# Hybrid streaming-encoder layer on one core: the convolution branch's two transpositions through DRAM with one contiguous store and four loads of 2 KB pieces each

## The chip, the core and the metric

The kernel runs on one core of a Trainium2 chip. TensorE (PE) multiplies matrices and transposes into PSUM, VectorE (DVE), ScalarE (ACT) and GpSimd (POOL) do the elementwise work, and SyncE (SP) issues most of the DMAs. Each engine carries out its own instructions in the order in which they were built; semaphores make one engine wait for another or for a DMA. The metric is the time in microseconds (us) of one execution of the program on the device; the median of several runs is compared. A profiled execution has its own time and a span, which is the stretch from the first to the last instruction that the trace shows.

## What is computed

One layer of a streaming encoder with 512 tokens and 1024 channels, in float32. Four token mixers (differential attention A, forgetting attention F, a convolution branch C, a short gated convolution D) share one input projection, are gated, summed and projected; cross-attention and a gated MLP follow. The change is in branch C:

```python
c_a, c_g = jnp.split(c_u + b_glu[l], 2, axis=-1)
yc = _dwconv_causal(c_a * jax.nn.sigmoid(c_g), conv_dw[l]) + conv_dw_b[l]   # 31 taps, 512 channels
yc = jax.nn.silu(_layer_norm(yc, conv_ln_g[l], conv_ln_b[l]))               # mean and variance over channels
...
br = jnp.stack([ya, yf, yc, ys], axis=2)
proj = jnp.einsum('bsnc,ncd->bsnd', br, w_branch[l])
```

The convolution runs along tokens, so channels lie on partitions; the layer norm needs sums over channels, so there tokens lie on partitions. The branch is turned twice: channels to tokens before the norm and back after it.

## The kernel before

Every matrix product is made of three float32r products (high part by high part, high by low, low by high), so each weight block is loaded by SP into one of two `wr` buffers (`load_raw`, L176), rounded to its high part `wh` by ACT (L190), and its low part `wl` is made by DVE (L191). `run_blocks` walks through a list of such blocks and keeps three of them ahead. A block is 24 products of 128x512 on PE. There are four `wh` and four `wl` buffers, so the cast of a block waits until PE has finished the block four places ahead of it.

Work that is not a weight block is written as generators (`bg.add`), which are advanced between blocks, up to two at a time; each yields a cost and a waiting time. `conv_norm_task` is one of them. The final order of the instructions on every engine is made when the kernel is built, by a scheduler that simulates the engines; on the chip that order is fixed.

Around the change the blocks on PE are, in this order: the last block of branch D's output (`y8b`), four blocks of the values of attention A (`v_jobs`: products into four PSUM banks, two tagged `av` and two tagged `mm`), then the query and key projections of the first head (`qk_jobs`, L772 to L786, into the two `mm` banks in turn) and of the second head, whose query block needs the bank of the first head's query block again. The values leave PSUM through ACT (high part, L155) and DVE (low part, L156), bank by bank.

`conv_norm_task` does this, once the four convolutions have ended (`conv_y`, a tile of 128 partitions by 4 blocks of 512 tokens; channel 128 j + p is block j of partition p):

1. Each of the two turns has four DVE instructions (L676) that transpose squares of 32 by 32 inside each of the four groups of 32 partitions, block by block, into the other 128x4x512 tile (`conv_u` for the first turn, `conv_y` for the second).
2. Four stores by SP (L680), each from 32 partitions, lay the squares out in a 512x512 DRAM tensor (`conv_tok`, `conv_chan`) so that its rows are whole. Each contiguous piece is 32 elements, 128 bytes.
3. Four loads by SP (L683), each of 128 rows of 2 KB into all 128 partitions, bring back 128 tokens (or channels) each into `xn`.
4. Between the turns, for each of the four blocks of tokens: `bn_stats` and `bn_aggr` on DVE (L693, L694), 1/sqrt on POOL (L268, L271), and the normalization on DVE (L696).
5. After the second turn, for each block j of channels: two ACT passes over `xn[:, j]` (L705, L706), a DVE pass (L707) and the split into high and low parts (L158, L159), into `y["c"]`.

`xn` takes one of the two buffers with the tag `qk`; the second head's query and key tile takes the same buffer afterwards (its first writer is the POOL memset, L772).

Of the kernel before, what the change touches and what calls it, by code (L numbers as in the profile page):

```python
# [17 lines left out]
F32 = mybir.dt.float32  # L18
F32R = mybir.dt.float32r
AF = mybir.ActivationFunctionType  # L20
ALU = mybir.AluOpType
# [4 lines left out]
P = 128  # L26
S = 512
D = 1024
NT = S // P
# [54 lines left out]
def hybrid_layer(ctx: ExitStack, tc: tile.TileContext, a: dict, out: bass.AP):  # L84
    nc = tc.nc
    V, A, G, PE, SP = nc.vector, nc.scalar, nc.gpsimd, nc.tensor, nc.sync
# [4 lines left out]
    dram = ctx.enter_context(tc.tile_pool(name="dr", bufs=1, space=DRAM))  # L91
# [39 lines left out]
    for i in range(8):  # L131
        n = ("wh", "wl")[i % 2]
# [3 lines left out]
        elif i < 6:  # L136
            n = ("fz_raw", "fz", "fe", "fu", "fd")[i - 1]
# [14 lines left out]
    def split(ps, hi, lo, scale=None):  # L152

        if scale is None:
            A.copy(hi, ps)  # L155
            V.tensor_tensor(lo, ps, hi.bitcast(F32), ALU.subtract)  # L156
        else:
            A.activation(hi, ps, AF.Copy if isinstance(scale, float) else AF.Identity, scale=scale)  # L158
            V.scalar_tensor_tensor(lo, ps, scale, hi.bitcast(F32), ALU.mult, ALU.subtract)  # L159
# [104 lines left out]
    def rstd_of(pool, parts, n=1):  # L264

        m = pool.tile([P, n], F32, tag="st_m", name="st_m", bufs=4)
        r = pool.tile([P, n], F32, tag="st_r", name="st_r", bufs=4)
        G.tensor_tensor(m, parts[0], eps[:, :n], ALU.add)  # L268
        for part in parts[1:]:
            G.tensor_tensor(m, m, part, ALU.add)  # L270
        G.tensor_tensor(r, m, nhalf[:, :n], ALU.pow)  # L271
        return r
# [40 lines left out]
    def e4(dtype=F32):  # L313
        return m1p.tile([P, 2, S], dtype, tag="e", name="e", bufs=3)
# [54 lines left out]
    where, rows, par = {}, [], []  # L369
    for i, plan in enumerate(plans):  # L370
        r_t = m1p.tile([P, P], F32, tag="fbias" if i == 2 else "ck", name=f"rows{i}", bufs=2)
        n = 0
# [116 lines left out]
    def pc(name, j=0, n=1):  # L489
        i, base = where[name]  # L490
        return par[i][:, base + j:base + j + n]
# [14 lines left out]
    half = {}  # L506
# [74 lines left out]
    def y8(dtype=F32R):  # L581
        return m2p.tile([P, 4, S], dtype, tag="y8", name="y8", bufs=2)
# [15 lines left out]
    conv_u, conv_y = y8(F32), y8(F32)  # L598
# [57 lines left out]
    def conv_task(j):  # L656
# [5 lines left out]
        for k in range(n - 1):  # L662
# [4 lines left out]
                conv_ends.append(ins.ins)  # L667
            yield 0.66, 0.0

    def conv_norm_task():  # L670
        xn = m1p.tile([P, 5, S], F32, tag="qk", name="xn", bufs=2)
        tok, chan = (dram.tile([S, S], F32, name=n) for n in ("conv_tok", "conv_chan"))

        def turn(rows, squares, src):
            for i in range(4):
                V.transpose(squares[:, i], src[:, i])  # L676
                yield 0.65, 0.0
            form = rows.rearrange("(b r) (j a c) -> a r j b c", r=32, a=4, c=32)
            for a in range(4):
                SP.dma_start(form[a], squares[a * 32:a * 32 + 32].rearrange("r j (b c) -> r j b c", c=32))  # L680
            yield 0.0, 4.0
            for i in range(4):
                SP.dma_start(xn[:, i], rows[i * P:(i + 1) * P, :])  # L683
            yield 0.0, 5.0

        yield 0.0, 2.0
        while len(conv_ends) < 4:
            yield 0.0, 0.5
        yield from turn(tok, conv_u, conv_y)
        for t in range(NT):  # L690
            st = m1p.tile([P, 6], F32, tag="bn6", name="bn6", bufs=2)
            mv = m1p.tile([P, 2], F32, tag="bn2", name="bn2", bufs=2)
            V.bn_stats(st, xn[:, t])  # L693
            V.bn_aggr(mv, st)  # L694
            r = rstd_of(m1p, [mv[:, 1:2]])
            V.tensor_scalar(xn[:, t], xn[:, t], mv[:, 0:1], r, ALU.subtract, ALU.mult)  # L696
            yield 1.5, 0.0
        yield from turn(chan, conv_y, xn)
        while "d" in y:
            yield 0.0, 2.0  # L700
        yield 0.0, 2.0
        y["c"] = (y8(), y8())
        for j in range(4):
            e = e4()
            A.activation(e[:, 0], xn[:, j], AF.Identity, bias=pc("ln_b", j), scale=pc("ln_g", j))  # L705
            A.activation(e[:, 1], xn[:, j], AF.Tanh, bias=half["ln_b"][:, j:j + 1], scale=half["ln_g"][:, j:j + 1])  # L706
            V.scalar_tensor_tensor(e[:, 0], e[:, 1], 1.0, e[:, 0], ALU.add, ALU.mult)  # L707
            split(e[:, 0], y["c"][0][:, j], y["c"][1][:, j], 0.5)
            yield 1.4, 1.0
# [364 lines left out]
    def mixer_jobs():  # L1074
        yield from c_jobs()
        yield then(lambda: bg.add(lam_task(), "lam"))
        yield from d_jobs()
        yield then(lambda: bg.add(conv_norm_task(), "conv"))
        wide = m1p.tile([P, NT, D], F32, tag="v", name="wide")
        free = iter([wide[:, i] for i in (0, 1, 2, 3) * 2])  # L1080
# [674 lines left out]
```

## Time and profile before

| | before |
| --- | --- |
| runs shown (us) | 1063.41, 1061.37, 1061.96; median 1061.96 |
| profiled execution, its own time (us) | 1061.46 |
| its span (us) | 1059.7 |
| mean granted TensorE clock | 0.998 |
| instructions in the span | 14546 |
| DMA traffic | 156.78 MB, mean 148 GB/s |

Times inside the trace count from the span's start. In an engine's rows, the number in brackets is idle time before the instruction and what ended it. A matmul's duration is modelled and longer than the distance to the next one, as matmuls are pipelined: two neighbouring 128x512 products stand 0.227 us apart, while each is given 0.39 us.

### The profile page before, as it was taken

What the parts mean: (1) busy time and instruction counts of PE and PEld (TensorE: products, weight loads), DVE (VectorE), ACT (ScalarE), POOL (GpSimd) and SP (SyncE); (2) the same over time, 40 slices, a digit from 0 to 9 for tenths busy, and PEclk for the clock granted to TensorE, in tenths of its full rate; (3) what the DMA queues carried; (4) which work ended last, traced back from release to release, by engine and by line L of the source; (5) the groups of instructions that cost most, each with busy time, mean ns of one, the idle gap of its engine ahead of it and who ended that gap; (6) DMA issues with size and microseconds to landing.
All of it is one profiled execution on the core that took longest, in us unless ns stands there. A gap on an engine that the chain in (4) does not pass through costs nothing.

```text
span 1059.7 us, 14546 instructions
## 1 busy us (share of the span) xinstructions
PE 1048.7 (99%) x5343; PEld 891.8 (84%) x5343; DVE 800.8 (76%) x1270; ACT 497.9 (47%) x819; POOL 150.8 (14%) x249
## 2 busy tenths in 40 slices
PE   9999999999999999999999999999999999999997
PEld 8888888878888988888888899999888888888886
DVE  6999997577666358766575888886778788777796
ACT  5322222277465255655443665654333333445672
POOL 4001000100001015322100031031111211111011
PEclk9999999999999999999999999999999999999999
DMA  8854335732222243322344734226566776725662
GB/s 269 300 153 104 104 97 128 198 113 80 80 80 68 59 135 100 97 84 80 120 140 154 268 133 120 80 81 199 179 229 211 235 230 209 236 80 179 210 216 80
DMA packets 179773, 156.78 MB, mean 148 GB/s; under 512 B 22207, under 2 KB 151852, under 8 KB 179701
## 3 DMA queue, kind: packets, MB, share of 16 engines
q1 hardware_dynamic: 170659, 124.10, 38.9%
q10 hardware_dynamic: 6482, 23.21, 5.8%
q0 software_dynamic: 2560, 8.54, 2.8%
q8 instruction: 42, 0.69, 0.3%
q14 instruction: 30, 0.25, 0.1%
HBM read 135.89 MB, written 19.94 MB: 147 GB/s over the span
## 4 chain that ended last, share of the span: by engine, by line
PE 95%; DMA 1%; DVE 1%; ACT 1%; issue 0%; POOL 0%; SPq 0%; POOLq 0%; DVEq 0%; ACTq 0%
PE ps_mm L232 51%; PE ps_av L232 29%; PE ps_sc L232 7%; PE ps_tr L232 4%; PE ps_tr L236 3%; DMA xn<-conv_tok 1%; PE ps_mm L442 1%; PE ps_av L442 1%; DMA conv_chan<-y 0%; PE ps_mm L384 0%; SPq L680 0%; PE ps_sc L389 0%; DMA xn<-conv_chan 0%; DVE wl L191 0%; POOL st_r L271 0%
## 5 line engine op out<-in xcount | busy, mean ns | idle before, releaser
L190 ACT CAST wh<-wr 128x1024 fp32r<-128x1024 f32 (+1 forms) x142 | 148.6, 1049 | 273.5 <-PE ps_mm L232 185.6
L191 DVE TENSOR_TENSOR wl<-wr,wh 128x1024 fp32r<-128x1024 f32 (+1 forms) x142 | 178.1, 1256 | 80.9 <-ACT wh L190 80.3
L232 PE MATMUL ps_mm<-hth,wh 128*128 128x512 f32 (+1 forms) x616 | 231.4, 382 | 2.4 <-DVE qk L777 1.9
L232 PE MATMUL ps_mm<-htl,wh 128*128 128x512 f32 (+1 forms) x616 | 230.1, 380 | 0.0
L232 PE MATMUL ps_mm<-hth,wl 128*128 128x512 f32 (+1 forms) x616 | 229.9, 380 | 0.0
L232 PEld LDWEIGHTS ps_mm<-hth,wh 128*128 128x128 f32 x616 | 114.1, 188 | 24.5 <-issue 2.3
L232 PEld LDWEIGHTS ps_mm<-hth,wl 128*128 128x128 f32 x616 | 114.0, 188 | 21.3
L232 PEld LDWEIGHTS ps_mm<-htl,wh 128*128 128x128 f32 x616 | 114.1, 188 | 20.3
L232 PE MATMUL ps_av<-htl,wh 128*128 128x512 f32 (+1 forms) x328 | 122.5, 373 | 0.0
L232 PE MATMUL ps_av<-hth,wh 128*128 128x512 f32 (+1 forms) x328 | 122.4, 373 | 0.0
L232 PE MATMUL ps_av<-hth,wl 128*128 128x512 f32 (+1 forms) x328 | 122.4, 373 | 0.0
L664 DVE SCALAR_TENSOR_TENSOR y<-y,par,y 128x482 f32<-128x482 f32 (+29 forms) x120 | 82.9, 727 | 0.2
L232 PEld LDWEIGHTS ps_av<-hth,wh 128*128 128x128 f32 x328 | 61.6, 188 | 10.9
L232 PEld LDWEIGHTS ps_av<-hth,wl 128*128 128x128 f32 x328 | 61.6, 188 | 10.9
L232 PEld LDWEIGHTS ps_av<-htl,wh 128*128 128x128 f32 x328 | 61.6, 188 | 10.8
L1548 DVE TENSOR_TENSOR wl<-dw,wh 128x1024 fp32r<-128x1024 f32 x32 | 40.2, 1260 | 13.2 <-ACT wh L1547 13.0
L1547 ACT CAST wh<-dw 128x1024 fp32r<-128x1024 f32 x32 | 33.4, 1051 | 23.3 <-PE ps_tr L232 8.5
L1002 POOL TENSOR_SCALAR fbias<-ck,cq 128x128 f32<-128x128 f32 (+3 forms) x32 | 27.5, 865 | 68.9 <-DVE st L1008 63.7
L1496 ACT ACTIVATE th<-c 128x512 f32<-128x512 f32 x22 | 13.9, 632 | 48.3 <-DVE c L594 48.2
L155 ACT CAST pth<-ps_tr 128x512 fp32r<-128x512 f32 (+3 forms) x56 | 23.4, 448 | 22.0 <-PE ps_tr L236 21.9
L594 DVE SCALAR_TENSOR_TENSOR c<-ps_mm,par,c 128x510 f32<-128x510 f32 (+1 forms) x44 | 32.7, 744 | 0.7
L156 DVE TENSOR_TENSOR ptl<-ps_tr,pth 128x512 fp32r<-128x512 f32 (+3 forms) x56 | 27.9, 513 | 6.1 <-ACT pth L155 5.9
(469 smaller groups left out, 2102.9 us busy)
## 6 DMA issues: line engine op xcount, KB each, us to landing
wr<-in_w_up SPq DMA_DIRECT2D x44, 512.0 KB
wr<-in_w_in SPq DMA_DIRECT2D x38, 512.0 KB
wr<-in_w_gate SPq DMA_DIRECT2D x32, 512.0 KB
wp<-in_w_down ACTq DMA_DIRECT2D x22, 512.0 KB
sums<-wp ACTq DMA_DIRECT2D x22, 512.0 KB
dw<-sums SPq DMA_DIRECT2D x44, 256.0 KB
wr<-in_w_branch SPq DMA_DIRECT2D x16, 512.0 KB
wide<-in_w_out SPq DMA_DIRECT2D x12, 512.0 KB
```

Of the source, the lines that this page charges most:

```text
L155: A.copy(hi, ps)
L156: V.tensor_tensor(lo, ps, hi.bitcast(F32), ALU.subtract)
L190: order(A.copy(hi, raw[:, :n]))
L191: low.tensor_tensor(lo, raw[:, :n], hi.bitcast(F32), ALU.subtract)
L232: PE.matmul(ps, lhs, rhs, start=start, stop=stop)
L236: PE.transpose(ps, x, ident[:n, :n])
L442: keep(PE.matmul(banks[c][:, :S // 2], w[p == 1][:, k, c * P:(c + 1) * P], ht[p == 2][:, i * 4 + k, :S // 2], start=(i, p, k) == (0, 0, 0) ...
L594: ins = V.scalar_tensor_tensor(dst[:, s:], src[:, :S - s], w(k), dst[:, s:], ALU.mult, ALU.add)
L664: ins = V.scalar_tensor_tensor(dst[:, s:], src[:, :S - s], pc("conv_dw", k * 4 + j), dst[:, s:], ALU.mult, ALU.add)
L1002: G.tensor_scalar(bias[:, :w], ck[j][:, :w], -1.0, cq[:, qt, head:head + 1], ALU.mult, ALU.add)
L1547: A.copy(hi, x)
L1548: V.tensor_tensor(lo, x, hi.bitcast(F32), ALU.subtract)
```

## The change

The squares are placed by the DVE transposition itself, in such an order that each partition's 2048 elements go to the DRAM tensor as one contiguous row of 8 KB; the tensor now has 128 rows of 2048. One store per turn replaces four. The four loads now differ by the 32 partitions that they write: each takes, for its 32 partitions, four pieces of 512 elements (2 KB) from rows 32 apart. `xn` then holds, on partition p, four blocks of 512 whose order is (block, token group, 32) instead of one block after the other, so `bn_stats`, the normalization and the two ACT passes read through strided views (`tokens[:, t]`, `turned_y[:, j]`); what they compute is the same. The transpositions of the first turn each write into all of `conv_u`; before, the one of block j wrote block j only. The same number of DVE and ACT instructions is issued; SP issues 10 DMAs in the two turns instead of 16. Two helper functions, `squares` and `turn`, are added that nothing calls.

```diff
 def conv_norm_task():
     xn = m1p.tile([P, 5, S], F32, tag="qk", name="xn", bufs=2)
-    tok, chan = (dram.tile([S, S], F32, name=n) for n in ("conv_tok", "conv_chan"))
-    def turn(rows, squares, src):
-        for i in range(4):
-            V.transpose(squares[:, i], src[:, i])
-            yield 0.65, 0.0
-        form = rows.rearrange("(b r) (j a c) -> a r j b c", r=32, a=4, c=32)
-        for a in range(4):
-            SP.dma_start(form[a], squares[a * 32:a * 32 + 32].rearrange("r j (b c) -> r j b c", c=32))
-        yield 0.0, 4.0
-        for i in range(4):
-            SP.dma_start(xn[:, i], rows[i * P:(i + 1) * P, :])
-        yield 0.0, 5.0
+    tok, chan = (dram.tile([P, NT * S], F32, name=n) for n in ("conv_tok", "conv_chan"))
...
-    yield from turn(tok, conv_u, conv_y)
+    sq = conv_u.rearrange("p j c -> p (j c)").rearrange("p (b t j c) -> p j t b c", b=4, t=NT, j=4)
+    for j in range(4):
+        V.transpose(sq[:, j], conv_y[:, j].rearrange("p (t b c) -> p t b c", t=NT, b=4))
+        yield 0.65, 0.0
+    SP.dma_start(tok, conv_u.rearrange("p j c -> p (j c)"))
+    yield 0.0, 4.0
+    form = tok.rearrange("(a r) (b x) -> b r a x", r=32, b=4)
+    for b in range(4):
+        SP.dma_start(xn[b * 32:b * 32 + 32, :4], form[b])
+    yield 0.0, 5.0
+    tokens = xn[:, :4].rearrange("p a (t x) -> p t a x", t=NT)
+    sq = conv_y.rearrange("p j c -> p (j c)").rearrange("p (a j t c) -> p t a j c", a=4, j=4, t=NT)
     for t in range(NT):
...
-        V.bn_stats(st, xn[:, t])
+        V.bn_stats(st, tokens[:, t])
...
-        V.tensor_scalar(xn[:, t], xn[:, t], mv[:, 0:1], r, ALU.subtract, ALU.mult)
+        V.tensor_scalar(tokens[:, t], tokens[:, t], mv[:, 0:1], r, ALU.subtract, ALU.mult)
         yield 1.5, 0.0
-    yield from turn(chan, conv_y, xn)
+    for t in range(NT):
+        V.transpose(sq[:, t], tokens[:, t].rearrange("p a (j c) -> p a j c", j=4))
+        yield 0.65, 0.0
+    SP.dma_start(chan, conv_y.rearrange("p j c -> p (j c)"))
+    yield 0.0, 4.0
+    form = chan.rearrange("(b r) (a x) -> a r b x", r=32, a=4)
+    for a_ in range(4):
+        SP.dma_start(xn[a_ * 32:a_ * 32 + 32, :4], form[a_])
+    yield 0.0, 5.0
+    turned_y = xn[:, :4].rearrange("p b (j t c) -> p j t b c", j=4, t=NT)
...
     for j in range(4):
         e = e4()
-        A.activation(e[:, 0], xn[:, j], AF.Identity, bias=pc("ln_b", j), scale=pc("ln_g", j))
-        A.activation(e[:, 1], xn[:, j], AF.Tanh, bias=half["ln_b"][:, j:j + 1], scale=half["ln_g"][:, j:j + 1])
+        one, two = (e[:, i].rearrange("p (t b c) -> p t b c", t=NT, b=4) for i in range(2))
+        A.activation(one, turned_y[:, j], AF.Identity, bias=pc("ln_b", j), scale=pc("ln_g", j))
+        A.activation(two, turned_y[:, j], AF.Tanh, bias=half["ln_b"][:, j:j + 1], scale=half["ln_g"][:, j:j + 1])
```

More of the change, by code (lines that the diff above doesn't have):

```diff
@@ L668, in conv_task, with squares, turn @@
             yield 0.66, 0.0
+    def squares(dst, src, n, b=4):
+        V.transpose(dst.rearrange("p (b n c) -> p n b c", b=b, c=32), src.rearrange("p (n b c) -> p n b c", b=b, c=32))
+    def turn(dst, src, n, between, name):
+        t = dram.tile([P, n * P], F32, name=name)
+        squares(between, src, n)
+        yield 0.1 + 0.14 * n, 0.5
+        SP.dma_start(t, between)
+        yield 0.0, 4.0
+        form = t.rearrange("(i r) (b x) -> b r i x", r=32, b=4)
+        for b in range(4):
+            SP.dma_start(dst[b * 32:b * 32 + 32].rearrange("r (i x) -> r i x", i=4), form[b])
+        yield 0.0, 5.0
     def conv_norm_task():
         xn = m1p.tile([P, 5, S], F32, tag="qk", name="xn", bufs=2)
-        tok, chan = (dram.tile([S, S], F32, name=n) for n in ("conv_tok", "conv_chan"))
-        def turn(rows, squares, src):
-            for i in range(4):
-                V.transpose(squares[:, i], src[:, i])
-                yield 0.65, 0.0
-            form = rows.rearrange("(b r) (j a c) -> a r j b c", r=32, a=4, c=32)
-            for a in range(4):
-                SP.dma_start(form[a], squares[a * 32:a * 32 + 32].rearrange("r j (b c) -> r j b c", c=32))
-            yield 0.0, 4.0
-            for i in range(4):
-                SP.dma_start(xn[:, i], rows[i * P:(i + 1) * P, :])
-            yield 0.0, 5.0
+        tok, chan = (dram.tile([P, NT * S], F32, name=n) for n in ("conv_tok", "conv_chan"))
         yield 0.0, 2.0
@@ L688, in conv_norm_task @@
             yield 0.0, 0.5
-        yield from turn(tok, conv_u, conv_y)
+        sq = conv_u.rearrange("p j c -> p (j c)").rearrange("p (b t j c) -> p j t b c", b=4, t=NT, j=4)
[5 more added lines that the diff above has]
+        form = tok.rearrange("(a r) (b x) -> b r a x", r=32, b=4)
+        for b in range(4):
+            SP.dma_start(xn[b * 32:b * 32 + 32, :4], form[b])
+        yield 0.0, 5.0
+        tokens = xn[:, :4].rearrange("p a (t x) -> p t a x", t=NT)
+        sq = conv_y.rearrange("p j c -> p (j c)").rearrange("p (a j t c) -> p t a j c", a=4, j=4, t=NT)
         for t in range(NT):
@@ L692, in conv_norm_task @@
             mv = m1p.tile([P, 2], F32, tag="bn2", name="bn2", bufs=2)
-            V.bn_stats(st, xn[:, t])
+            V.bn_stats(st, tokens[:, t])
             V.bn_aggr(mv, st)
             r = rstd_of(m1p, [mv[:, 1:2]])
-            V.tensor_scalar(xn[:, t], xn[:, t], mv[:, 0:1], r, ALU.subtract, ALU.mult)
+            V.tensor_scalar(tokens[:, t], tokens[:, t], mv[:, 0:1], r, ALU.subtract, ALU.mult)
             yield 1.5, 0.0
-        yield from turn(chan, conv_y, xn)
+        for t in range(NT):
+            V.transpose(sq[:, t], tokens[:, t].rearrange("p a (j c) -> p a j c", j=4))
+            yield 0.65, 0.0
+        SP.dma_start(chan, conv_y.rearrange("p j c -> p (j c)"))
+        yield 0.0, 4.0
+        form = chan.rearrange("(b r) (a x) -> a r b x", r=32, a=4)
+        for a_ in range(4):
+            SP.dma_start(xn[a_ * 32:a_ * 32 + 32, :4], form[a_])
+        yield 0.0, 5.0
+        turned_y = xn[:, :4].rearrange("p b (j t c) -> p j t b c", j=4, t=NT)
         while "d" in y:
```

## The prediction

> **What bounds the kernel now.** I read the busy times first, then where the bounding engine idles, then what ends that idling, and last the stretch of the change instruction by instruction.
>
> ```profile
> span 1059.7 us, 14546 instructions
> ...
> PE 1048.7 (99%) x5343; PEld 891.8 (84%) x5343; DVE 800.8 (76%) x1270; ACT 497.9 (47%) x819; POOL 150.8 (14%) x249
> ```
>
> PE is busy for all but 11 us. The busy time of PE by stretches shows where those lie:
>
> ```profile
> 0.00:150.00 150.00, 148.41 (x750) 125.51 (x751) 137.93 (x210) 49.81 (x68) 15.61 (x32) 1.00 0.58 178
> 150.00:215.00 65.00, 65.00 (x288) 53.68 (x286) 45.73 (x66) 19.93 (x25) 3.14 (x8) 1.00 0.61 153
> 215.00:230.00 15.00, 12.94 (x58) 10.30 (x58) 11.61 (x20) 12.21 (x19) 1.04 (x2) 1.00 0.39 110
> 230.00:900.00 670.00, 669.59 (x3568) 575.75 (x3567) 484.50 (x839) 335.23 (x605) 113.11 (x183) 1.00 0.43 137
> 900.00:1060.00 160.00, 152.71 (x685) 126.60 (x683) 121.07 (x139) 80.74 (x106) 17.94 (x24) 0.98 0.51 166
> ```
>
> 1.6 us stand at the start, 7.3 at the end, 0.4 in between, and 2.06 us between 215 and 230 us. Only the last is near the change. In the order of time it is two stalls, beside the product that opens the first head's query block (209.62), which doesn't wait:
>
> ```profile
> 209.62 0.39 PE L232 MATMUL ps_mm<-hth,wh 128*128 128x512 f32 x1
> ...
> 214.84 0.39 PE L232 MATMUL ps_mm<-hth,wl 128*128 128x512 f32 x1
> 215.41 0.50 PE L232 MATMUL ps_mm<-hth,wh 128*128 128x512 f32 x1 [0.19 <-DVE v L156]
> ...
> 220.76 0.39 PE L232 MATMUL ps_mm<-hth,wl 128*128 128x512 f32 x1
> 223.02 0.47 PE L232 MATMUL ps_mm<-hth,wh 128*128 128x512 f32 x1 [1.87 <-DVE qk L777]
> ```
>
> Neighbours stand 0.227 us apart, so 215.41 - 214.84 - 0.23 = 0.34 us and 223.02 - 220.76 - 0.23 = 2.03 us are lost: 2.4 us in all. That is the most that this branch can give back, 0.2% of the time, and as PE hardly idles until the tail, any stall that is added here is added to the end in full. ACT's rows say why PE stalls:
>
> ```profile
> 204.38 1.05 ACT L190 CAST wh<-wr 128x1024 fp32r<-128x1024 f32 x1 [4.39 <-PE ps_mm L232]
> ...
> 211.09 0.81 ACT L705 ACTIVATE e<-xn,par 128x512 f32<-128x512 f32 x1 [2.04 <-DMA xn<-conv_chan]
> ...
> 213.94 0.56 ACT L155 CAST v<-ps_mm 128x512 fp32r<-128x512 f32 x1
> 214.40 1.05 ACT L190 CAST wh<-wr 128x1024 fp32r<-128x1024 f32 x1
> ...
> 219.76 0.81 ACT L705 ACTIVATE e<-xn,par 128x512 f32<-128x512 f32 x1
> ...
> 221.30 0.58 ACT L776 CAST qk<-ps_mm 64x512 fp32r<-64x512 f32 x1
> ```
>
> ACT waits for the load of the second turn until 211.09 with the eviction of the fourth value bank behind it, which comes at 213.94, though PE left that bank as the next block began (209.62); later two of the branch's passes (219.76) stand ahead of the query block's second eviction (221.30). Both stalls are the late end of the two turns, seen by PE through ACT's order.
>
> **The two turns, priced.** SP's and DVE's rows give the legs:
>
> ```profile
> 177.31 4.62 SPq L680 DMA_DIRECT2D conv_tok<-y  x4
> 182.02 3.08 SPq L176 DMA_DIRECT2D wr<-in_w_in  x2
> 185.35 2.75 SPq L683 DMA_DIRECT2D xn<-conv_tok  x4
> ...
> 199.87 5.41 SPq L680 DMA_DIRECT2D conv_chan<-y  x4
> 205.38 1.26 SPq L176 DMA_DIRECT2D wr<-in_w_in  x1
> 208.52 1.77 SPq L683 DMA_DIRECT2D xn<-conv_chan  x4
> ```
>
> ```profile
> 176.57 0.71 DVE L676 STREAM_TRANSPOSE y<-y 128x512 f32<-128x512 f32 x1
> ...
> 188.14 0.69 DVE L1053 SCALAR_TENSOR_TENSOR acc<-ge,ps_mm 128x512 f32<-128x512 f32 x1 [2.11 <-PE ps_mm L232]
> ...
> 191.22 1.41 DVE L693 BATCH_NORM_STATS2 bn<-xn 128x6 f32<-128x512 f32 x2 [1.08 <-DMA xn<-conv_tok]
> ...
> 198.54 1.30 DVE L676 STREAM_TRANSPOSE y<-xn 128x512 f32<-128x512 f32 x2
> ...
> 214.67 0.68 DVE L156 TENSOR_TENSOR v<-ps_mm,v 128x512 fp32r<-128x512 f32 x1
> ```
>
> Before: the stores take 8.04 us (177.31 to 185.35) and 8.65 us (199.87 to 208.52); the loads 5.87 us (185.35 to 191.22) for 1.57 MB (1.05 MB and the weight block issued just ahead), and 2.57 us (208.52 to 211.09) for the first 0.26 MB, which was all that the first ACT pass needed. The last two numbers are one line: 1.31 MB more took 3.30 us, which is 397 GB/s, with 1.9 us fixed. The rates of three stretches:
>
> ```profile
> 178.50:185.00 6.50, 6.50 (x31) 5.37 (x30) 1.99 (x2) 1.74 (x3) 0.00 (x0) 1.00 1.11 177
> 190.00:191.00 1.00, 1.00 (x6) 0.84 (x5) 0.14 (x1) 0.00 (x0) 0.00 (x0) 1.00 1.05 401
> 222.00:223.00 1.00, 0.00 (x0) 0.01 (x1) 0.86 (x3) 1.00 (x2) 0.48 (x1) 1.00 1.10 331
> ```
>
> The first is mostly the 128 byte stores, the second the loads of 2 KB pieces into 128 partitions, the third a weight block of 512 byte pieces, also into 128.
>
> *Start.* DVE is packed to 177.28 (176.57 + 0.71). Three transpositions move from earlier to behind the last convolution step, because each now writes into all of `conv_u`, which that step still reads. That is work moved within a full engine, so it costs nothing until a new wait appears: a PSUM addition (L1053) is reached earlier than PE can release it. I take 177.6, between 177.3 and 178.1.
>
> *Store.* One DMA of 8 KB rows over 128 partitions. Bounds: 1.9 + 1.05/0.397 = 4.55 us and today's 8.04 to 8.65; I take 4.55, since its rows are longer than those of the 401 GB/s stretch. It saves some 3.5 to 4 us a turn.
>
> *Loads.* Still 2 KB pieces, but each load writes 32 partitions, and the first reader now needs all four, as each load carries a quarter of every token group and channel block. Below, the bound is 4.55 us; above, the rate of the stores, which also touch 32 partitions each: 1.9 + 1.05/0.177 = 7.8 us. I take the stores' rate raised by what long pieces gain over short ones (401/331): 214 GB/s, hence 1.9 + 4.9 = 6.8 us. I stay near the stores because the partition count is what the change gives the loads in common with them. The Trainium skill speaks against the change here: "SBUF — State Buffer", section "Door 1: The DMA port swizzle", says that a transfer's rate goes by how many of 16 ports its partitions reach, that 32 partitions reach eight, and gives 189 GB/s for them against 328 for 128 (1 MiB). By that figure the leg would be an estimated 1.9 + 5.5 = 7.4 us; no row before shows 2 KB pieces into 32 partitions.
>
> *Between the turns.* 191.22 to 199.84 is 8.62 us; in the changed order one L1053 (0.69) falls inside: 9.3.
>
> *ACT.* The order of the changed kernel, fixed when it is built, is around here (numbers of the changed text; L730 and L731 are the old L705 and L706):
>
> ```
> L190 (four weight casts), L730, L731, L730, L731, L730, L731, L155 v, L155 v, L158, L155 v, L158, L155 v, L190
> ```
>
> Three pairs of passes now come ahead of all four value evictions, and behind the cast that PE released at 204.38, so they can't start before 205.4. Let E be their start. Six passes take 4.28 us (211.09 to 213.94 is four); the first eviction 0.46, the second 0.59, its low part on DVE behind the first one's: PE gets the bank of the query block at E + 6.2. Two blocks of 24 x 0.227 later, at E + 17.1, the second head's query block starts; before it did at 223.02. The later evictions (fourth value bank at E + 8.3, query at about E + 14) are ready in time, so both old stalls vanish and one new one at 209.62 stands in their place. The shift of the end is E - 205.9.
>
> *Sum.* E = 177.6 + 4.6 + load + 9.3 + 4.6 + load = 196.1 + 2 x load = 209.7 with 6.8. The shift is +3.8 us. What the waits hold up meanwhile: on DVE, behind the first batch-norm (177.6 + 4.6 + 6.8 = 189.0), the L1053 that frees the fourth value bank, done by 191.1; the order has PE write that bank 24 products after the one that L1053 waits for (188.1), at 193.5, so 2.4 us cover it, and 1.4 at a load leg of 7.8. On SP, behind each store's landing, the loads and then a weight block; blocks are cast only when PE frees a buffer (the 4.39 us of ACT's first row), which covers about 4 us. DVE's and ACT's work count is unchanged. 1061.46 + 3.8 = 1065.3 for the profiled execution, which lies 0.5 below the median of the runs shown; between the two I say **1065.5 us**.
>
> **Rivals.** *(a) Full rate, not slower.* The four loads run one behind the other at the 397 GB/s of the loads before: 4.55 each turn, E = 205.2, held to 205.4 by the cast, shift -0.5: **1061.0**. For it: same piece size, and the trace has no proof that partitions matter, since 128 byte pieces alone could explain 177. Against it: nothing there shows a fast transfer of 32 partitions. It decides where a load leg is under 4.9 us (350 GB/s); above, the change is slower than before. Even here the gain stays under 2 us, as ACT's order keeps a stall of 2 us at 209.62.
>
> *(b) The strided walks cost DVE or ACT time.* Transpositions now write, and in the second turn read, runs of 32 elements. The nearest rows:
>
> ```profile
> L156 DVE TENSOR_TENSOR v<-ps_av,v x6: 415/424/692, 206.6 to 373.7; 128x256 fp32r<-128x256 f32 x4, 128x512 fp32r<-128x512 f32 x2
> L156 DVE TENSOR_TENSOR xql<-ps_mm,xqh x4: 410/416/418, 649.9 to 670.7; 128x256 fp32r<-128x256 f32 x4
> ```
>
> 256 elements written in runs of 64 take 424 ns, unbroken 416, so I book nothing. Were transpositions to take twice as long, each turn starts 2.5 us later: E + 5, **1070.3**.
>
> *(c) The stores stay slow.* If 8 KB rows brought nothing, E rises by 7.3: 1072.6. The 401 GB/s speak against it.
>
> **How the numbers follow.** A change within 0.2% (2.1 us) is about what a measurement of this kernel can't tell from none. Forecast 0.56; (a) 0.29; (b) 0.06; (c) 0.02; faster by something unseen here 0.07, which would need both stalls gone and none new. The forecast's own range is 1063.5 to 1068 (load legs of 6 to 7.8 us). Faster 0.07; same 0.34, which is (a) and the forecast's lower edge; slower 0.59. Range 1060.8 to 1068.2, from (a) to the stores' rate.
>
> **What will show it.** Right: the store's leg near 4.6 us in SP's rows; the first batch-norm and the first ACT pass waiting for loads for 6 us or more; the first pass near 209 to 210; one PE stall of 6 to 7 us ahead of the query block, released by DVE's L156, and none at the next two blocks; nothing changed after that. Wrong: DMA rates above 350 GB/s in the load legs, the first pass at 205.4, a stall of 2 us; or DVE's transpositions longer than 0.7 us; or PE losing time elsewhere.

## The result, and the profile after

The kernel became slower. Four runs each give a median of 1068.78 us (1068.51 to 1069.14) against 1062.24 us (1061.37 to 1063.41), a ratio of 1.0061 (95% interval 1.0048 to 1.0075). The profiled execution took 1069.14 us, 7.7 more than the one before. The busy times and the same stretches as before (us; then busy time of PE, PE's weight loads, DVE, ACT and POOL with counts; the granted TensorE clock, the busy share of the DMA engines, GB/s):

```profile
span 1067.4 us, 14539 instructions
...
PE 1050.5 (98%) x5343; PEld 893.4 (84%) x5343; DVE 799.6 (75%) x1270; ACT 497.9 (47%) x819; POOL 149.8 (14%) x249
```

```profile
150.00:215.00 65.00, 60.09 (x266) 49.43 (x264) 43.25 (x63) 18.45 (x22) 3.95 (x8) 0.99 0.57 156
215.00:230.00 15.00, 12.62 (x43) 10.15 (x44) 9.77 (x14) 8.99 (x15) 1.04 (x2) 0.72 0.17 44
230.00:900.00 670.00, 669.73 (x3574) 576.20 (x3573) 481.66 (x840) 336.95 (x607) 112.68 (x182) 1.00 0.44 136
```

From 230 to 900 us PE idles no more than before. Between 150 and 215 us PE now idles 4.9 us, and from 215 to 230 us it is as busy as before (12.62 against 12.94 us) but carries out 43 products instead of 58, at a granted clock of 0.72. The turns, in the rows of SP, DVE and ACT (a store leg runs from the store's issue to the first load's, a load leg from there to the first instruction that reads the loaded data):

```profile
177.82 0.34 SPq L697 DMA_DIRECT2D conv_tok<-y  x1
179.60 0.37 SPq L176 DMA_DIRECT2D wr<-in_w_in  x1
181.97 1.77 SPq L701 DMA_DIRECT2D xn<-conv_tok  x4
...
199.22 0.34 SPq L716 DMA_DIRECT2D conv_chan<-y  x1
200.32 0.37 SPq L176 DMA_DIRECT2D wr<-in_w_in  x1
203.55 1.75 SPq L720 DMA_DIRECT2D xn<-conv_chan  x4
```

```profile
175.31 2.49 DVE L695 STREAM_TRANSPOSE y<-y 128x512 f32<-128x512 f32 x4
...
190.34 1.29 DVE L708 BATCH_NORM_STATS2 bn<-xn 128x6 f32<-128x512 f32 x2 [4.00 <-DMA xn<-conv_tok]
```

```profile
211.06 0.81 ACT L730 ACTIVATE e<-xn,par 128x512 f32<-128x512 f32 x1 [4.59 <-DMA xn<-conv_chan]
...
215.31 0.56 ACT L155 CAST v<-ps_av 128x512 fp32r<-128x512 f32 x1
215.78 0.58 ACT L155 CAST v<-ps_mm 128x512 fp32r<-128x512 f32 x1
```

The store legs are 4.15 and 4.33 us (177.82 to 181.97, 199.22 to 203.55), half of the old 8.04 and 8.65. The load legs are 8.37 us (181.97 to 190.34) and 7.51 us (203.55 to 211.06), and they eat up what the stores gave: the first pass comes at 211.06, as before (211.09). But before, two pairs of passes stood ahead of the fourth value eviction alone; now three pairs stand ahead of all four on ACT, and the first eviction starts at 215.31. PE in the order of time:

```profile
209.70 0.39 PE L232 MATMUL ps_mm<-wh,htl 128*128 128x512 f32 x1
217.38 0.80 PE L232 MATMUL ps_mm<-hth,wh 128*128 128x512 f32 x1 [7.29 <-DVE v L156]
217.97 0.63 PE L232 MATMUL ps_mm<-htl,wh 128*128 128x512 f32 x1
...
223.09 0.57 PE L232 MATMUL ps_mm<-htl,wh 128*128 128x512 f32 x1
223.50 0.40 PE L232 MATMUL ps_mm<-hth,wl 128*128 128x512 f32 x1
223.74 0.40 PE L232 MATMUL ps_mm<-hth,wh 128*128 128x512 f32 x1
```

One stall of 7.45 us (217.38 - 209.70 - 0.23) stands ahead of the query block. Behind it come twelve steps of 0.427 us from 217.97 to 223.09, and only from 223.50 on are products 0.23 us apart again: 14 products took 6.12 us where they take 3.18, another 2.94 us lost. The granted clock says the same:

```profile
212.00:213.00 1.00, 0.00 (x0) 0.00 (x0) 0.39 (x1) 1.00 (x2) 0.00 (x0) 1.00 1.19 291
213.00:214.00 1.00, 0.00 (x0) 0.00 (x0) 0.31 (x1) 1.00 (x3) 0.00 (x0) 0.61 0.43 104
214.00:223.00 9.00, 5.62 (x13) 4.46 (x14) 7.56 (x12) 7.88 (x13) 1.04 (x2) 0.50 0.05 14
223.00:224.00 1.00, 1.00 (x5) 0.73 (x5) 0.45 (x1) 0.00 (x0) 0.00 (x0) 0.77 1.09 329
```

It halves some 3.3 us into the idle time (209.93 to about 213.2) and comes back 6.1 us after PE has resumed.

### The profile page after: what moved, and what is told of

It is laid out like the page before. It is cut to its first block, busy times and chain, and to the rows that moved or that the text cites. A ratio compares the mean times of both kernels' runs of the same rounds, so it can differ in the third digit from the quotient of the medians.

```text
span 1067.4 us, 14539 instructions
## 1 busy us (share of the span) xinstructions
PE 1050.5 (98%) x5343; PEld 893.4 (84%) x5343; DVE 799.6 (75%) x1270; ACT 497.9 (47%) x819; POOL 149.8 (14%) x249
## 4 chain that ended last, share of the span: by engine, by line
PE 93%; DMA 3%; DVE 1%; ACT 1%; issue 1%; POOL 0%; SPq 0%; POOLq 0%; DVEq 0%; ACTq 0%
PE ps_mm L232 51%; PE ps_av L232 28%; PE ps_sc L232 7%; PE ps_tr L232 4%; PE ps_tr L236 3%; DMA xn<-conv_tok 1%; DMA xn<-conv_chan 1%; DMA wide<-in_w_out 1%; DMA conv_chan<-y 0%; DMA wr<-in_w_in 0%; DMA conv_tok<-y 0%; DMA xs<-in_x 0%; ACT e L731 0%; DVE nt L281 0%; POOL st_r L271 0%
```

## The experiments

The theory after this profile, with the letters of the expectations: (A) loads into 32 partitions each are slow; (C) the long stall costs TensorE's clock as well; (D) what reaches the end is set by where the late passes stand on ACT's queue. The rivals: the new walk over the DRAM tensor or the weight blocks beside the loads are what is slow (B), the slow products cover another wait, and a late branch C delays something else.

**Loads of 32 partitions in the kernel before.** Layout, stores and passes as before; each load takes four pieces of 2 KB for 32 partitions.

```diff
-            for i in range(4):
-                SP.dma_start(xn[:, i], rows[i * P:(i + 1) * P, :])
+            form = rows.rearrange("(i b r) c -> b r i c", b=4, r=32)
+            for b in range(4):
+                SP.dma_start(xn[b * 32:b * 32 + 32, :4], form[b])
```

> The kernel before, with its own 128 byte stores, but each of the four loads of a turn now writes 32 partitions (four 2 KB pieces each) instead of one block of all 128. The computation is unchanged. Theory A (a transfer into 32 partitions runs at about half the rate of one into 128): the first turn's load leg grows from 5.87 us to 7.5 us or more, and the second turn's, until ACT's first pass, to 7 us or more (all four loads are needed now). In this kernel's order ACT's passes stand behind the four value evictions and ahead of the first query evictions, so the stall moves to the second head's query block: 5 to 6 us, time 3 to 6 us above before. Rival B (the legs of the changed kernel are long because of the weight blocks beside them and because of the 8 KB pitch of the DRAM rows): legs of 5.9 and 4.6 us, time within 1 us of before.

1074.17 us (two runs), ratio 1.0115 (1.0094 to 1.0135). The rows of DVE (first turn), SP, ACT and PE of this kernel:

```profile
196.29 1.29 DVE L694 BATCH_NORM_STATS2 bn<-xn 128x6 f32<-128x512 f32 x2 [5.88 <-DMA xn<-conv_tok]
```

```profile
212.93 0.33 SPq L684 DMA_DIRECT2D xn<-conv_chan  x1
```

```profile
222.20 0.81 ACT L706 ACTIVATE e<-xn,par 128x512 f32<-128x512 f32 x1 [5.97 <-DMA xn<-conv_chan]
```

```profile
231.58 0.47 PE L232 MATMUL ps_sc<-qk 128*128 128x128 f32 x1 [10.65 <-ACT qk L786]
```

The first load leg is 10.61 us (185.68 to 196.29) in place of 5.87, the second 9.27 us (212.93 to 222.20), without any new layout; both also hold bytes of weight blocks that were issued ahead. Its passes stand behind the value evictions, but three pairs stand ahead of the query and key casts, and PE loses its time at the first scores (10.65 us). The place and the size were not those expected (5 to 6 us at the second head's query block, 3 to 6 us in all; it became 12 us). So it is the loads' form that is slow, and the place of the passes on ACT decides where PE pays.

**Loads of 128 partitions in the kernel after.** The contiguous store stays; each load takes one 2 KB piece of every row into all partitions. The data then lands in other places of `xn`, so this kernel leaves out the right values of branch C; it serves for its times only.

```diff
-            SP.dma_start(xn[b * 32:b * 32 + 32, :4], form[b])
+            SP.dma_start(xn[:, b], tok[:, b * S:(b + 1) * S])
...
-            SP.dma_start(xn[a_ * 32:a_ * 32 + 32, :4], form[a_])
+            SP.dma_start(xn[:, a_], chan[:, a_ * S:(a_ + 1) * S])
```

> The changed kernel, but each of the four loads of a turn writes one 2 KB piece to each of all 128 partitions, from DRAM rows of the same 8 KB pitch; the data lands in other places of xn, so branch C's values are not the reference's. The order on ACT, DVE and SP is that of the changed kernel. Theory A: load legs of 4.6 to 6 us, the first ACT pass at 205.4 to 207, a PE stall of 2 to 3.5 us and no fall of the clock, time 1061 to 1063. Rival B: legs stay at 7.5 to 8.4 us, time 1068 to 1069.

1066.26 us (1064.67 to 1068.39), ratio 1.0044 (1.0027 to 1.0060). SP's and ACT's rows of the second turn, and PE's row at the query block:

```profile
201.35 1.82 SPq L718 DMA_DIRECT2D xn<-conv_chan  x4
```

```profile
207.42 0.81 ACT L728 ACTIVATE e<-xn,par 128x512 f32<-128x512 f32 x1 [1.85 <-DMA xn<-conv_chan]
```

```profile
213.74 0.79 PE L232 MATMUL ps_mm<-hth,wh 128*128 128x512 f32 x1 [3.82 <-DVE v L156]
```

The legs are 5.95 us (181.80 to 187.75) and 6.07 us, as theory A says: the same bytes in the same pieces cost 1.4 to 2.4 us less a turn when every load reaches all partitions. The time was expected at 1061 to 1063 and came out higher, because a stall of 3.82 us was already enough to lower the clock: it is 0.50 from 212.7 to 219.5 us, and products stand 0.43 us apart until about 219.5.

**The order of the loads.** Groups 0, 2, 1, 3 instead of 0, 1, 2, 3.

```diff
-        for b in range(4):
+        for b in (0, 2, 1, 3):
...
-        for a_ in range(4):
+        for a_ in (0, 2, 1, 3):
```

> The kernel after, with the four loads of each turn issued for the partition groups 0, 2, 1, 3 and not 0, 1, 2, 3; nothing else moves. If groups that lie side by side share what they are slow at (the way into their 32 partitions), loads of distant groups that are in flight together overlap better: legs of 6 to 6.5 us in place of 8.4 and 7.5, the first query block 3 to 4 us earlier, and 1063 to 1065 us. If the loads run one behind the other, or if the shortage is not by neighbouring groups, the legs stay at 7.5 to 8.4 us and the time at 1068 to 1069.

One run of 1069.13 us. Legs 7.40 us (181.96 to 189.36) and 7.12 us (203.73 to 210.85), against 7.5 to 8.4 in the other profiles with this layout: 0.1 and 0.4 us below the shortest of them, where 6 to 6.5 us would have spoken for neighbouring groups. In this one run they are at most a small part of the cause. What makes 32 partitions slow, the port, the queue or something else, stays open.

**Keeping PE busy through the stall.** 30 products that nobody reads, between the value block and the query block.

```diff
                     if kb == 3:
                         split(st["ps"][t], dst[0][0][:, t], dst[0][1][:, t])
+                if kb == 3:
+                    spare = bank("sc")
+                    for _ in range(30):
+                        keep(PE.matmul(spare, ht[0][:, 0, :P], ht[0][:, 0, :], start=True, stop=True))
```

> The changed kernel with 30 products of 128x512 into an unused PSUM bank placed on PE between the last value block and the first query block (6.8 us of extra PE work whose result nobody reads), where PE otherwise idles for 7.5 us. The other engines' order is unchanged. Theory C (the idle time made the granted clock fall to half for the first 6 us of the query block, which costs 2.7 us by itself): clock 1.00 throughout, the query block starts at 217.4 as before and its products stand 0.227 us apart at once, time 2.5 to 2.9 us below the changed kernel, about 1066. Rival (the slow products come from something else, such as the DMA traffic or the bank, and idling doesn't matter): time unchanged or longer.

1069.71 us (1066.88 to 1070.51), ratio 1.0068 (1.0050 to 1.0085): no gain in the median. In its profile the clock is 1.00 from 200 to 245 us and the query block runs at once at full pace, but at 400 us PE waits again, and behind that wait its products stand 0.427 us apart once more:

```profile
401.38 0.50 PE L232 MATMUL ps_sc<-qk 128*128 128x256 f32 x2 [1.93 <-DVE st L1037]
...
402.53 0.63 PE L232 MATMUL ps_mm<-htl,wh 128*128 128x512 f32 x1
...
405.92 0.39 PE L232 MATMUL ps_mm<-hth,wh 128*128 128x512 f32 x1
```

The clock is 0.50 there from 402.5 to 405.9 us, after waits of only 1.93 and 0.32 us. As the filling takes one score bank out of turn, it was repeated with 14 products into each of the two banks:

> The kernel after, with 28 products of 128x512 that nobody reads on TensorE between the value block and the first head's query block (two turns of 14 into two score banks, so that the rotation of these two banks is as before; the first fill took one bank). At 0.227 us each they fill 6.4 of the 7.45 us in which TensorE stood. Clock theory: the clock stays at 1.00 from 200 to 230 us, the query block still starts at about 217 us, its products come 0.227 us apart at once, and the 2.9 us lost after the stall come back: about 1066 us (1065.5 to 1066.5). Rival: the slow products are a cover for something that is late anyway, so that a wait of the same size appears behind them: 1068 to 1069 us. If the first fill's time (1069.7) came from its odd number of banks, this one ends below it by 3 us or more; if from the filling itself, at the same time.

1068.70 us (1066.65 to 1071.50), ratio 1.0065 (1.0042 to 1.0089), with a new wait of 1.6 us at 400 us too, behind which the clock stays at 1.00. What happens there is seen on POOL, which stores the gates' running sums (`crows`) and loads them back (`ck`). First the kernel after, then the evenly filled one:

```profile
394.69 0.57 POOL L980 DMA_DIRECT2D crows<-e  x1 [30.57 <-DVE e L979]
397.20 1.12 POOL L997 DMA_DIRECT2D ck<-crows  x2 [1.94 <-DMA crows<-e]
...
411.73 0.58 POOL L997 DMA_DIRECT2D ck<-crows  x1
```

```profile
391.15 0.57 POOL L985 DMA_DIRECT2D crows<-e  x1 [30.58 <-DVE e L984]
395.16 1.11 POOL L1002 DMA_DIRECT2D ck<-crows  x2 [3.43 <-DMA crows<-e]
...
410.90 0.58 POOL L1002 DMA_DIRECT2D ck<-crows  x1
```

The filled kernel arrives 3.54 us ahead (391.15 against 394.69) and leaves 0.83 ahead, because the store was answered after 3.43 us instead of 1.94, and the loads behind it took longer too. In the second half of that wait no byte moved; these are two stretches of the filled kernel:

```profile
391.10:393.10 2.00, 2.00 (x11) 1.66 (x9) 0.57 (x1) 0.19 (x1) 0.57 (x1) 1.00 0.75 222
393.10:395.10 2.00, 2.00 (x15) 1.70 (x14) 1.30 (x2) 1.44 (x2) 0.00 (x0) 1.00 0.00 0
```

Whether that answer is chance was asked with more runs, beside the kernel after itself:

> The kernel after with the 28 products between the value block and the first query block once more, in more rounds. In the two filled profiles TensorE was 3.4 us ahead of the kernel after from 242 to 390 us and lost 2.5 us at 400 us, where the gate rows go to memory and back (the first store answered after 3.43 us in place of 1.94, its bytes having moved at the usual moment). If that slow answer is chance, the times of this kernel fall into two groups, and the lower one is 2.5 to 3.5 us under the kernel after: its lowest runs at 1065.5 to 1066.9, and a profile with an answer under 2 us shows 1066 us. If the slow answer belongs to this kernel, or the clock is worth nothing, the median stays within 0.7 us of the kernel after's of this call and the lowest runs with it.

> The kernel after itself, unchanged, for its scatter beside that of the filled kernel on the same chip: 1068.5 to 1069.2 us as in its first four runs; if the answer at 400 us is sometimes slow here too, some runs 1 to 2.5 us above.

The kernel after: 1069.02 us (1067.18 to 1070.13), ratio 1.0067 (1.0054 to 1.0080). The filled one: 1067.29 us in the profiled run and 1069.97 to 1071.06 in the five others; median 1070.73, ratio 1.0079 (1.0066 to 1.0093). The profile of the 1067.29 us run has the quick answer (392.09 to 394.51 on POOL, 1.85 us of waiting), and PE at the query block:

```profile
210.05 6.51 PE L789 MATMUL ps_sc<-hth 128*128 128x512 f32 x28
217.64 0.50 PE L232 MATMUL ps_mm<-hth,wh 128*128 128x512 f32 x1 [1.08 <-DVE v L156]
...
218.44 0.39 PE L232 MATMUL ps_mm<-hth,wh 128*128 128x512 f32 x1
```

Beside the profiled repeat of the kernel after (query block at 216.73, 1069.05 us) it starts the query block 0.91 us later and ends 1.76 us earlier: 2.7 us regained, nearly the 2.94 counted. So in this profile the clock's cost came back up to the end; in the median of the six runs it did not. That most runs of the filled kernel lie 3 us higher fits the slow answer of the two profiles that have it, but those runs were not profiled. The filling is not needed for a slow answer: the kernel after with its passes held behind the key casts, shown below, has one of 3.70 us. What makes it slow stays open.

**Holding all passes behind the query casts.** All four pairs on ACT behind the first head's two query casts:

```diff
+        while len(first_query) < 2:
+            yield 0.0, 0.5
         for j in range(4):
...
+            with tc.issue_after(first_query[1]):
                 A.activation(one, turned_y[:, j], AF.Identity, bias=pc("ln_b", j), scale=pc("ln_g", j))
...
```

> The changed kernel with branch C's ACT passes (and what follows them) placed behind the first head's query evictions in ACT's order, so that value and query evictions never wait for the second turn's loads. Theory D (the time went only through ACT's order: evictions queued behind a pass that waits for the loads): load legs as long as in the changed kernel, no PE stall at the query blocks, clock 1.00, time 2 to 2.5 us below before, about 1060. Rival (the late branch is needed soon after anyway, so the wait reappears at the second head's blocks or at branch C's gate blocks): time 1063 or more.

1064.51 us (1063.69 to 1067.65), ratio 1.0028 (1.0016 to 1.0040). The stall at the query block is gone with load legs nearly as long as before the edit (7.74 us for the first, 181.39 to 189.13). A new one stands at the first scores, as the waits of PE between 200 and 240 us show:

```profile
PE ps_sc L232 <- ACT qk L813: 2.7, 1, 2.7
PE ps_sc L232 <- DVE qk L814: 0.3, 1, 0.3
```

The clock falls behind these waits as well: it is 0.50 from 230.3 to 233.7 us, while PE works. By an estimate from these figures that is 1.7 us, half of 3.41; with 3.0 us of waits, and without the 2.4 us that the kernel before loses here, it makes 2.3 of the 2.6 us measured against 1061.95. The rival was right that the time stays above 1063 us; the wait came at another place than it named.

**Holding them behind the key casts**, in the kernel after and in the kernel before. The same edit, with the key casts as the mark:

> The kernel after, with ScalarE's eight passes over the turned squares held behind the first head's four key casts on ScalarE (the first hold put them behind the query casts only, and the wait moved to the key casts). If all that the late loads cost comes through the evictions that stand behind the passes on ScalarE, then neither the query blocks nor the first scores wait: no stall over 0.5 us on TensorE between 200 and 235 us, clock 1.00 there, and 1060 to 1062 us. Rival: the passes (8 of 0.8 us, with the casts between them) now stand ahead of the second head's evictions, or branch c's blocks come too early for them: a stall of 1.5 to 3 us moves there and the time stays at 1063.5 to 1065.

> The kernel before, with the same hold: the eight passes behind the first head's key casts. Before's two stalls of 0.34 and 2.03 us come from the same queue, so they should go: 1059.7 to 1060.5 us, and nothing else. If this is as fast as the kernel after with the hold, the layout of the squares is worth nothing either way once the passes wait for the right thing. Rival: the two stalls are only moved: 1062 us as before.

Both got slower: 1070.67 us (1069.72 to 1072.89), ratio 1.0073 (1.0055 to 1.0091), and 1069.91 us (1068.18 to 1070.78), ratio 1.0067 (1.0051 to 1.0082). For the kernel after the rival was right in kind, and the loss was larger than it said; for the kernel before neither expectation held, as both saw it at 1062 us or less. ACT's rows of the first of them:

```profile
237.18 0.80 ACT L734 ACTIVATE e<-xn,s_ln_b,s_ln_g 128x512 f32<-128x512 f32 x1
238.01 0.58 ACT L804 CAST qk<-ps_mm 64x512 fp32r<-64x512 f32 x1
```

The second head's query cast follows the last pass directly: its tile takes the buffer of `xn`, which the passes read. PE waits 4.8 and 1.6 us for it, in both kernels, and the clock is 0.50 for 10.2 us in both. The passes thus have a latest place as well as an earliest.

**Two pairs behind the query casts, two behind the key casts**, in both kernels.

```diff
+            while len(marks) < 2 + j // 2 * 2:
+                yield 0.0, 0.5
             e = e4()
...
+            with tc.issue_after(marks[1 + j // 2 * 2]):
                 A.activation(one, turned_y[:, j], AF.Identity, bias=pc("ln_b", j), scale=pc("ln_g", j))
...
```

> The kernel after, with two of the four pairs of passes on ScalarE held behind the first head's query casts and two behind its key casts. The passes read a buffer that the second head's queries take over, so they must be done before those are cast (holding all of them behind the key casts made the second head wait 4.8 us); in two halves each fits between two blocks of 5.4 us on TensorE. If the loss of the kernel after is only the place of the passes on ScalarE's queue, TensorE has no wait over 0.6 us between 200 and 240 us, its clock stays 1.00, and the time is 1060.5 to 1062.5 us. Rival: nine microseconds of ScalarE's work land between evictions in any order, and a wait of 1.5 to 3 us stays: 1063.5 to 1065.

> The kernel before with the same two holds. If the kernel before waits 0.34 and 2.03 us for the same reason, they go: 1059.7 to 1060.5 us, and then the old and the new layout differ by less than 1 us when the passes are out of the way. Rival: the old layout's turn ends 1.6 us later than the new one's where both are held (its four stores are slower), so that the first pair comes too late for its gap: 1062 us as before.

The kernel after with this order: 1061.37 us (1060.15 to 1062.46, 11 runs), ratio to the kernel before 0.9996 (0.9987 to 1.0004). ACT's rows around the passes, then all waits of PE between 200 and 240 us:

```profile
209.45 0.59 ACT L155 CAST v<-ps_mm 128x512 fp32r<-128x512 f32 x1 [0.77 <-PE ps_mm L232]
...
217.73 0.58 ACT L804 CAST qk<-ps_mm 64x512 fp32r<-64x512 f32 x1 [1.53 <-DVE qk L805]
218.34 0.82 ACT L733 ACTIVATE e<-xn,par 128x512 f32<-128x512 f32 x1
...
222.24 0.58 ACT L812 CAST qk<-ps_mm 64x512 fp32r<-64x512 f32 x1
...
225.70 0.81 ACT L733 ACTIVATE e<-xn,par 128x512 f32<-128x512 f32 x1
```

```profile
PE ps_mm L232 <- DVE qk L805: 0.6, 1, 0.6
PE ps_sc L232 <- DVE qk L814: 0.5, 1, 0.5
PE ps_tr L236 <- DVE e L881: 0.2, 1, 0.2
```

The first load leg is 7.83 us (181.29 to 189.12), as slow as ever, the passes start at 218.34, seven microseconds later than in the kernel after, and its whole loss is gone. The kernel before with the same order took 1063.36 us (1061.13 to 1064.65, 11 runs), ratio 1.0013 (1.0005 to 1.0022). In its profile ACT waits 4.69 us for a weight block just before the query casts, which come 1.6 us later than in the other (217.25 against 215.62). That the old turn's longer occupation of SP delays that block is a guess. No version is clearly faster than the kernel before; the new layout in the split order is level with it. In that same order the old layout took 2.0 us more than the new one, and the intervals of the two ratios do not meet: with the passes out of the way the new layout is not the slower one.

## Why the prediction was off

It said 1065.5 us, slower. The direction was right, and so was the mechanism as far as the stall ahead of the query block; what PE does behind that stall was not. The time lies 3.3 us above the forecast. E is the start of the first ACT pass, as in the prediction.

- *The old stalls vanish*: right. The only stall left between 215 and 230 us is the new one.
- *Start and stores*: right. 177.82 against 177.6; legs of 4.15 and 4.33 us against 4.55 (4.6 in the sum), so 0.7 us better together. Rival (c) is out.
- *Loads*: right in kind, too small a term. 8.37 and 7.51 us against 6.8, 2.3 us more together, and the first lies above the upper bound of 7.8. That bound came from the mixed rate of the old stores; the row shows no limit, as the second leg of the kernel before with loads of this form took 9.27 us. The 7.4 us that the prediction gave beside its sum was nearer than the 6.8 in it. Rival (a) is out: from 185 to 190 us the DMAs move 211 GB/s, where it needed 350.
- *Between the turns*: 8.88 us (190.34 to 199.22) against 9.3. Transpositions took 0.62 us each (2.49 for four) and the first ACT pass 0.81 us, so the strided walks cost nothing and rival (b) is out.
- *The first pass*: 211.06 against 209.7. The terms add up: +0.2 start, +2.3 loads, -0.7 stores, -0.4 between the turns. That it came within 1.4 us is in part luck, as errors of both signs met.
- *ACT's order*: right, and the most useful step. The query block came at E + 6.32 us against E + 6.2. The split order shows the cause: the passes, with the DVE and ACT work that follows each, were moved, PE's order around them stayed the same, and the loss went.
- *"Two blocks of 24 x 0.227 later"*: this step failed. It took PE's pace behind the stall to be the one ahead of it. The clock had halved, and 14 products took 2.94 us longer. The prediction's row has a clock of 1.00 over the old 2.03 us stall, and it carried that over to one of 6 us.

Together 1.4 us of late passes and 2.9 us of clock make 4.3 us; the profiled execution ended 7.7 us later than before instead of 3.8. The missing -0.4 us is less than two executions of one kernel differ by (1061.37 to 1063.41).

A rule of the Trainium skill says just what was left out: "TensorE: Matmul & The Clock Gate", "Part 1: The HAM clock gate (the "warmup" mystery)", has PE fall to half its clock after an idle window of about 3.4 us, and return after about as much sustained work. The trace agrees on the half (0.427 against 0.227 us a product) and, in this profile, on the fall (3.3 us into the idle time); the return took longer here, 6.1 us. In two other profiles the fall came with less idle time: behind a wait of 2.66 us, with one of 0.31 us after it, in the kernel with its passes held behind the query casts, and behind 1.93 and 0.32 us in the first filled kernel.

## What to carry to other kernels

A branch that ends late costs what stands behind its first consumer on an in-order queue, so look at that engine's order before speeding up the branch: here moving eight passes was worth 7.7 us (1069.02 to 1061.37), with the load legs as long as ever. The latest place is set by buffers: the passes had to be done before the next user of theirs, the second head's queries. When a forecast has a stall on TensorE, add the slow restart to it: half of the time in which PE works at half clock. Here, between 200 and 900 us, every wait from 2.66 us up lowered the clock. Waits of about 2 us lowered it in one profile (1.93 us, with 0.32 us after it) and left it alone in three (2.03 us in the kernel before; 1.6 and 1.7 us, with 0.3 us after each).

## What was not expected of the hardware

- The slow restart lasted 6.1 us after the 7.45 us stall and cost 2.94 us. In the nine profiles whose clock fell between 200 and 410 us, it stayed at 0.50 for 3.4 us (twice), 6.8, 10.2 (five times) and 13.7 us: always a whole multiple of 3.41 us. In the 3.41 us ahead of each fall PE was busy for 0 to 1.3 us, and in the last 3.41 us ahead of each return for all of them.
- Four loads of 2 KB pieces took 7.1 to 8.4 us for 1.05 MB when each wrote 32 partitions (9.27 and 10.61 us beside the old stores), and 5.95 to 6.07 us when each wrote all 128, other traffic included.
- A small store was answered 1.84 to 1.94 us after its wait began in eleven profiles and 3.43 to 3.70 in three, with no bytes moving in the difference; in one of these a lead of 3.54 us shrank to 0.83.
